# A hybrid decoder layer on one core: the three attention patterns are combined in another tile and a step later, and one sample row moves from the projection to the output stage

## The chip, the core and the metric

The kernel runs on one core of a Trainium2 chip. The core has five engines with a queue each: TensorE (PE in the profile, with its weight loads as PEld), VectorE (DVE), ScalarE (ACT), GpSimd (POOL), and SyncE (SP), which here issues nearly all DMAs. Each queue is worked off in order: an instruction, or a DMA issue, that waits holds up everything behind it on its engine. The metric is the device time of one execution in microseconds (us).

## What is computed

One layer over a prompt of 4096 positions (model width 1024) and 8 sample sequences of 4 new tokens each. Cut to what matters here:

```
q,k,v,g_att,x_lru,g_lru = split(x @ w_in)              # one input projection
for (window, dilation) in (128,1), (512,4), (2048,16): # 8 heads of 64, 129 keys each
    o_i, m_i, den_i = windowed attention, keys gathered by stride
w_i   = den_i * exp(m_i - max m);  y_att = sum(w_i * o_i) / sum(w_i)
h     = RG-LRU scan over a width-4 convolution of x_lru
y     = LayerNorm(alpha * x + [y_att*silu(g_att) ; h*silu(g_lru)] @ w_out)
sample tokens: the same, with 2048 cached K and V rows per sequence
```

## The kernel before

The program is written out in order by hand, with four stages. Matrix products of full accuracy are made of three matmuls on a high and a low part.

**Projection** (`phase1`, to about 580 us). For each of 8 pieces of 512 positions, q and k are made in four groups each (`qk_group`, 24 matmuls into one PSUM bank, emptied by ACT at L204 and DVE at L205), then v. After each group `decode_step` adds a piece of work for the sample tokens: the cached keys of one sequence and one pattern are loaded (`dec_load`, 1 MB, or 256 KB for the stride-1 pattern p = 2), multiplied by q on DVE (L375), summed (L380) and saved. `early` = 5 of the 8 sequences are done here, 15 pieces, one every 1.6 groups. `early` also says how many are left for the output stage.

**Attention** (`phase2`, to about 1475 us). 384 steps; a unit of 48 steps does one pair of heads over half the prompt. A unit has four stretches of 512 positions, nb = 0 to 3. A step issues scores (L562, L563), transposes (L582) of the step two before, and products with v (L598), with about four matmuls of another projection (`filler`) between. For the strides 4 and 16, q is gathered by POOL three steps ahead (`gather_q`, L512, tile `qg`, four buffers). When a stretch is complete, a chain of work follows for it, each piece at a lag in steps (`k.lag`): the softmax statistics go out to DRAM (`stats_out`, tiles s4d, s1d) and come back in another layout (`stats_in`, tile ac), DVE makes the weights (`weights`, `weights_b`), they go out (`weights_c`, wd), come back spread over all partitions (`spread`, tile gb, L657, one buffer), and POOL combines (`combine`): five operations of 128x512 spread over four steps, the first at L670, the others run from the step loop at L855. Then `store` (L674) writes the result to DRAM (ad), from gb, by a DMA that POOL issues. `spread` waits on SP until gb is free. The o of the stride-16 pattern lies in u16 (two buffers), that of the strides 4 and 1 in the tiles u1 and u2.

**Recurrence** (`phase3`, to about 1950 us) is not touched.

**Output** (`phase4`). 32 blocks of 48 matmuls (L1341), 8 ticks apart; `at(tick, ...)` sets the order of all else between them. Here the remaining sequences' keys are multiplied (L1494) and summed (L1498), from tick `k_start` on, `k_step` ticks each, and for each of two groups of four sequences a softmax `soft1` to `soft6` runs from `soft_at`: `soft2` transposes the scores on PE into the tile ds (L1507), `soft3` and `soft4` work on DVE and ACT (L1515 to L1526), `soft5` transposes back on PE (L1531). `tail_mm` puts the last recurrent state into PSUM under the same tag ds, and `tail_out` copies it out on ACT.

Of the kernel before, what the change touches and what calls it, by code (L numbers as in the profile page):

```python
# [23 lines left out]
SPAN = 512  # L24
# [6 lines left out]
class Kern:  # L31
# [125 lines left out]
    def phase1(self, xs_ctx):  # L157
# [227 lines left out]
        for n, (b, p) in enumerate([(b, p) for b in range(self.early) for p in (2, 0, 1)]):  # L385
            g = 1.6 * n
            for d, f in ((0, dec_load), (1.6, dec_mul), (2.4, dec_sum), (3.4, dec_save)):
                decode.setdefault(int(g + d), []).append((f, b, p))
            if p == 2:
                decode.setdefault(int(g + (0.2 if b else 0)), []).append((row_q, b))  # L390
        order = dec_mul, row_q, dec_sum, dec_save, dec_load
# [60 lines left out]
    def phase2(self):  # L452
# [137 lines left out]
        def back(x):  # L590
# [10 lines left out]
            if x.b == 3:  # L601
                if x.pat == 0:
                    nc.scalar.copy(x.unit.u16.rearrange("p (i r) -> p r i", r=16)[:, 4 * x.a:4 * x.a + 4],
                                   o.rearrange("p (r i) -> p r i", r=4))
                else:
                    t = up.tile([128, SPAN], F32, tag=f"u{x.pat}", name="u", bufs=1 + x.pat)
                    if x.pat == 1:
                        nc.scalar.copy(t.rearrange("p (m r) -> p r m", r=4), o.rearrange("p (r m) -> p r m", r=4))
                    else:
                        nc.scalar.copy(t, o)  # L610
                    x.unit.u[x.pat, x.a] = t
# [14 lines left out]
        def weights(un, nb):  # L626
            r = slice(nb * 32, nb * 32 + 32)
            ac = un.ac[r].rearrange("p k a h s -> p s k (a h)")
            w = sp.tile([128, 3, 32], F32, tag="w", name="w")
            m = sp.tile([128, 32], F32, tag="wm", name="wm")  # L630
            un.w[nb] = w, m
# [4 lines left out]
        def weights_b(un, nb):  # L636
            r = slice(nb * 32, nb * 32 + 32)
            ac = un.ac[r].rearrange("p k a h s -> p s k (a h)")
            w, m = un.w.pop(nb)
            g = sp.tile([128, 3, 2, 16], F32, tag="wg", name="wg")  # L640
            nc.vector.tensor_mul(ac[:, 1], w[r], ac[:, 1])
# [19 lines left out]
        def combine(un, nb):  # L661
            s, gb = slice(nb * SPAN, (nb + 1) * SPAN), un.gb[nb]
            e = nc.gpsimd
            for k, (f, o, y) in enumerate(((e.tensor_mul, 1, un.u[1, nb]), (e.tensor_mul, 0, un.u16[:, s]),
                                           (e.tensor_mul, 2, un.u[2, nb]), (e.tensor_add, 0, gb[:, 1]),
                                           (e.tensor_add, 0, gb[:, 2]))):
                if k:
                    defer(min(k, 3), f, gb[:, o], gb[:, o], y)
                else:
                    f(gb[:, o], gb[:, o], y)  # L670
            defer(3, store, un, nb)

        def store(un, nb):
            nc.gpsimd.dma_start(out=dap(self.ad, un.c * 128 * SEQ + un.st0 * ST + nb * SPAN, [[SEQ, 128], [1, SPAN]]),  # L674
                                in_=un.gb.pop(nb)[:, 0])

# [8 lines left out]
        def gate_mul(th, p, t, j):  # L685
            nc.vector.scalar_tensor_tensor(th, th, 1.0, p, op0=ALU.add, op1=ALU.mult)
            freed[0] += 1
            defer(1, gate_store, th, t, j)

# [655 lines left out]
    def phase4(self):  # L1345
# [258 lines left out]
        at(10.4, tables2)  # L1604
        at(12, tail_mm)
        at(13, tail_out)
        start = {b: 8 * b for b in range(n_b)}
# [70 lines left out]
def tile_hymba_dilated_attn_rglru(ctx, tc, ins, outs):  # L1678
    k = Kern(ctx, tc, ins, outs)
    k.pr = 0.2, 5.5, 7.0  # L1680
    k.p2 = 6, 9, 5, 1, 1, 3, 4, 3, 6, 11, 12, 15, 19, 24, 24, 24, 24, 17, 381, 387, 3.95
    k.kl, k.lag, k.f0, k.wl, k.fill_rate = k.p2[:7], k.p2[7:13], k.p2[13:18], k.p2[18:20] + (2,), (k.p2[20],) * 8
# [11 lines left out]
    k.e0, k.e1, k.e2, k.smp = 4, (2,), (9,), (5, 14)  # L1694
    k.early, k.k_start, k.k_step, k.soft_at, k.v_step = 5, 16.0, 24.0, (12.0, 112.0), (24.0, 22.0)
    xs = k.xs_ctx = ExitStack()
# [34 lines left out]
```

## Time and profile before

| | us |
|---|---|
| median of 3 runs (lowest, highest) | 2373.68 (2371.04, 2378.28) |
| the profiled execution | 2381.04 |
| its span, first to last instruction | 2379.3 |
| PE busy in it | 2202.8 (93%) |
| DVE busy | 1417.2 (60%) |
| ACT busy | 1091.8 (46%) |
| POOL busy | 528.7 (22%) |

The mean granted TensorE clock was 0.963 of 2.4 GHz; it stands either at 2.4 or at 1.2 GHz, so a mean below 1 says in which share of a stretch it was down. The profiled execution is 7.4 us above the median of the three runs. The span is a chain of four stages, so what is won in one shifts all that follow; a share over the whole span says little about a stage.

### The profile page before, as it was taken

To read this page: it belongs to the slowest core of one execution; us is meant where nothing else is said; L and a number is where in the kernel's file an instruction comes from. 1 tells how busy PE (TensorE), PEld (TensorE's weight loads), DVE (VectorE), ACT (ScalarE), POOL (GpSimd) and SP (SyncE) were. 2 spreads that over 40 slices of the span, in tenths; PEclk is the share of its full clock that TensorE was granted. 3 is DMA by queue.
4 is the path that set the end of the run, shared out by engine and by line. 5 is a ranking of instruction groups with operands and counts; after the bars stand their busy time and mean duration, and the time that the engine had idled before them with its cause. 6 is when DMAs were issued, how large, how long until landed. Compare 5 with 4: busy or idle time off the path is not lost.

```text
span 2379.3 us, 42567 instructions
## 1 busy us (share of the span) xinstructions
PE 2202.8 (93%) x15274; PEld 1903.2 (80%) x15274; DVE 1417.2 (60%) x3544; ACT 1091.8 (46%) x2819; POOL 528.7 (22%) x499
## 2 busy tenths in 40 slices
PE   6999999999799889989998988699999989999998
PEld 5887778888688779878887977699999976777776
DVE  4355553322366767656665745477878878855555
ACT  3211212222466557656665765376777752122221
POOL 1000000000337375564746475200000000000000
PEclk9999999999899999989999988899999999999999
DMA  6867776647957877777687855445555557655531
GB/s 175 255 231 222 253 231 221 203 169 222 237 130 182 182 194 176 197 186 183 176 195 194 177 160 141 142 153 151 168 164 187 164 177 282 219 198 185 203 131 58
DMA packets 325491, 444.68 MB, mean 187 GB/s; under 512 B 60836, under 2 KB 196004, under 8 KB 320160
## 3 DMA queue, kind: packets, MB, share of 16 engines
q1 hardware_dynamic: 322560, 433.04, 62.8%
q0 software_dynamic: 2720, 8.92, 1.1%
q8 instruction: 122, 2.00, 0.4%
q14 instruction: 89, 0.73, 0.1%
HBM read 306.04 MB, written 135.85 MB: 186 GB/s over the span
## 4 chain that ended last, share of the span: by engine, by line
PE 60%; DMA 14%; POOL 6%; DVE 5%; issue 3%; ACT 3%; SPq 2%; ACTq 0%; POOLq 0%; DVEq 0%
PE po L1341 15%; PE o L598 4%; PE pt L582 4%; DMA gb<-wd 4%; PE pp L190 4%; POOL gb L855 3%; POOL qg L512 3%; PE s L562 2%; PE pg L1019 2%; PE pg L1021 2%; PE pg L1020 2%; PE xl L140 2%; PE xl L144 2%; PE xl L142 2%; PE pp L317 2%
## 5 line engine op out<-in xcount | busy, mean ns | idle before, releaser
L512 POOL CAST qg<-S 128x512 fp32r<-128x512 f32 x256 | 277.0, 1102 | 639.8 <-DMA S<-qd 501.3
L1341 PE MATMUL po<-S,mx 128*128 128x512 f32 x1536 | 370.9, 401 | 4.0 <-DVE S L129 3.5
L1341 PEld LDWEIGHTS po<-S,mx 128*128 128x128 f32 x1536 | 290.1, 190 | 88.9 <-issue 11.2
L569 DVE CUSTOM_DVE_ANT_0 sm<-s,mask 128x256 f32<-128x256 f32 (+1 forms) x768 | 269.7, 389 | 101.7 <-PE s L563 86.5
L573 ACT ACTIVATE sm<-sm,st 128x256 f32<-128x256 f32 (+1 forms) x512 | 251.6, 493 | 166.0 <-DVE st L569 131.8
L586 DVE COPY pts<-pt 128x512 f32<-128x512 f32 x228 | 156.9, 688 | 158.6 <-PE pt L582 156.6
L582 PE MATMUL pt<-ident,sm 128*128 128x128 f32 x1368 | 230.9, 288 | 0.3 <-ACT sm L573 0.2
L598 PE MATMUL o<-pts,v 128*64 128x128 f32 x2736 | 202.3, 289 | 23.5 <-DMA v<-vd 22.4
L562 PE MATMUL s<-S,qg 128*128 128x256 f32 x512 | 164.1, 340 | 48.4 <-POOL qg L512 39.6
L598 PEld LDWEIGHTS o<-pts,v 128*64 128x64 f32 x2736 | 152.3, 142 | 52.9 <-DMA v<-vd 25.2
L190 PE MATMUL pp<-S,xh 128*128 128x512 f32 x768 | 179.4, 394 | 12.8 <-DVE stg L205 6.3
L582 PEld LDWEIGHTS pt<-ident,sm 128*128 128x128 f32 x1368 | 155.6, 144 | 36.0 <-issue 17.7
L190 PEld LDWEIGHTS pp<-S,xh 128*128 128x128 f32 x768 | 145.3, 190 | 45.4 <-DVE stg L205 7.2
L316 PE MATMUL pp<-xh,S 128*128 128x512 f32 x448 | 177.2, 396 | 3.6 <-ACT xh L114 3.6
L317 PE MATMUL pp<-xh,S 128*128 128x512 f32 x448 | 176.2, 393 | 1.6 <-DVE xh L115 1.6
L318 PE MATMUL pp<-xh,S 128*128 128x512 f32 x448 | 175.3, 391 | 0.0
L573 ACT ACTIVATE sm<-sm,ac 128x128 f32<-128x128 f32 (+1 forms) x256 | 114.3, 448 | 104.1 <-DVE ac L569 103.1
L707 PE MATMUL f<-xh,S 128*128 128x256 f32 x512 | 149.3, 292 | 5.2 <-DMA xh<-xtd 5.2
L140 PE MATMUL xl<-xh,S 128*128 128x256 f32 x512 | 147.6, 288 | 6.1 <-DMA xh<-xtd 4.1
L562 PEld LDWEIGHTS s<-S,qg 128*128 128x128 f32 x512 | 102.6, 200 | 59.3 <-POOL qg L512 52.6
L144 PE MATMUL xl<-xh,S 128*128 128x256 f32 x512 | 147.3, 288 | 2.6 <-DVE S L129 2.1
L712 PE MATMUL f<-xh,S 128*128 128x256 f32 x512 | 148.7, 290 | 0.0
(289 smaller groups left out, 5106.7 us busy)
## 6 DMA issues: line engine op xcount, KB each, us to landing
xh<-xtd SPq DMA_DIRECT2D x256, 256.0 KB
S<-qd SPq DMA_DIRECT2D x128, 256.0 KB
xtd<-xh SPq DMA_DIRECT2D x56, 512.0 KB
gb<-wd SPq DMA_DIRECT2D x64, 384.0 KB
v<-vd SPq DMA_DIRECT2D x264, 64.0 KB
S<-kd SPq DMA_DIRECT2D x64, 256.0 KB
xr<-in_x_prompt_dram SPq DMA_DIRECT2D x32, 512.0 KB
arena<-in_cache_v_dram SPq DMA_DIRECT2D x16, 1024.0 KB
```

Of the source, the lines that this page charges most:

```text
L140: nc.tensor.matmul(out, wh, xh, start=(c == 0), stop=False)
L144: nc.tensor.matmul(out, wl, xh, start=False, stop=(c == k - 1))
L190: nc.tensor.matmul(p, l, m, start=(c == 0 and a + b == 0), stop=(c == 7 and (a, b) == ((1, 0) if j < 2 else (0, 1))))
L316: nc.tensor.matmul(ps, wh, xh, start=(c == 0), stop=False)
L317: nc.tensor.matmul(ps, wh, xl, start=False, stop=False)
L512: nc.gpsimd.tensor_copy(o, q.bitcast(F32))
L562: nc.tensor.matmul(s[:, h], q_ap(x, h, 0), k, start=True, stop=False)
L569: nc.vector.tensor_tensor_reduce(x.sm[:, h, o], s[:, h, i], self.mask[:, x.pat, o], -0.125, 3e38, ALU.add, ALU.min, x.stat[:, h, 0:1])
L573: nc.scalar.activation(x.sm[:, h, o], x.sm[:, h, o], AF.Exp, bias=x.stat[:, h, 0:1], scale=-1.0, accum_out=x.stat[:, h, 1:2])
L582: nc.tensor.transpose(p[:, h, kb], x.sm[:, h, kb * 128:(kb + 1) * 128], self.ident)
L598: nc.tensor.matmul(o[h * 64:(h + 1) * 64, x.b * 128:(x.b + 1) * 128], v[:, h * 64:(h + 1) * 64], x.pt[:, h, kb], start=(kb == kbs[0]), sto ...
L1341: self.nc.tensor.matmul(ps[j], l, self.Wo[j][c][:, s], start=(c == 0 and s == 0 and l is mh), stop=(c == 7 and l is ml))
```

## The change

In the attention stage the combination is formed in u16 (its slice of 512 positions) instead of gb, and the store reads u16; gb is last read by the second addition. Three lags are one step longer: `stats_in` 7 (6), `spread` 16 (15), `combine` 20 (19). The tile u1 has three buffers instead of two, and three small tiles of the weights one instead of two. `gate_store` comes two steps after `gate_mul` instead of one. In the projection, four sequences (12 pieces) are decoded instead of five, one piece every two groups, the multiplication one group after the load. In the output stage four sequences' keys remain instead of three, from tick 10, every 22 ticks (16, every 24); the two softmaxes begin at 14 and 114 (12 and 112); `tail_mm` and `tail_out` go from 12 and 13 to 60 and 61.

```diff
@@ phase1
-            g = 1.6 * n
-            for d, f in ((0, dec_load), (1.6, dec_mul), (2.4, dec_sum), (3.4, dec_save)):
+            g = 2 * n
+            for d, f in ((0, dec_load), (1, dec_mul), (2, dec_sum), (3, dec_save)):
...
@@ phase2, back
-                    t = up.tile([128, SPAN], F32, tag=f"u{x.pat}", name="u", bufs=1 + x.pat)
+                    t = up.tile([128, SPAN], F32, tag=f"u{x.pat}", name="u", bufs=3)
@@ weights (wm and, in weights_b, wg in the same way)
-            w = sp.tile([128, 3, 32], F32, tag="w", name="w")
+            w = sp.tile([128, 3, 32], F32, tag="w", name="w", bufs=1)
...
@@ combine, store
-            s, gb = slice(nb * SPAN, (nb + 1) * SPAN), un.gb[nb]
-            e = nc.gpsimd
-            for k, (f, o, y) in enumerate(((e.tensor_mul, 1, un.u[1, nb]), (e.tensor_mul, 0, un.u16[:, s]),
-                                           (e.tensor_mul, 2, un.u[2, nb]), (e.tensor_add, 0, gb[:, 1]),
-                                           (e.tensor_add, 0, gb[:, 2]))):
+            gb, e = un.gb.pop(nb), nc.gpsimd
+            o = un.u16[:, nb * SPAN:(nb + 1) * SPAN]
+            for k, (f, *a) in enumerate(((e.tensor_mul, gb[:, 1], gb[:, 1], un.u[1, nb]), (e.tensor_mul, o, o, gb[:, 0]),
+                                         (e.tensor_mul, gb[:, 2], gb[:, 2], un.u[2, nb]),
+                                         (e.tensor_add, o, o, gb[:, 1]), (e.tensor_add, o, o, gb[:, 2]))):
...
             nc.gpsimd.dma_start(out=dap(self.ad, ...),
-                                in_=un.gb.pop(nb)[:, 0])
+                                in_=un.u16[:, nb * SPAN:(nb + 1) * SPAN])
@@ gate_mul
-            defer(1, gate_store, th, t, j)
+            defer(2, gate_store, th, t, j)
@@ phase4
-        at(12, tail_mm)
-        at(13, tail_out)
+        at(60, tail_mm)
+        at(61, tail_out)
@@ numbers (k.lag is the 8th to the 13th of k.p2)
-    k.p2 = 6, 9, 5, 1, 1, 3, 4, 3, 6, 11, 12, 15, 19, 24, 24, 24, 24, 17, 381, 387, 3.95
+    k.p2 = 6, 9, 5, 1, 1, 3, 4, 3, 7, 11, 12, 16, 20, 24, 24, 24, 24, 17, 381, 387, 3.95
-    k.early, k.k_start, k.k_step, k.soft_at, k.v_step = 5, 16.0, 24.0, (12.0, 112.0), (24.0, 22.0)
+    k.early, k.k_start, k.k_step, k.soft_at, k.v_step = 4, 10.0, 22.0, (14.0, 114.0), (24.0, 22.0)
```

What this moves on SP, around the first combination of a unit (wd: weights out, ac: statistics of the next stretch in, gb: the spread, L484 the v of stride 4, L446 the next q). Before:

```order
L649 DMA wd<-wg 32x6x16
L75 DMA xh<-xtd 128x512
L623 DMA ac<-s4d 32x64
L623 DMA ac<-s1d 32x64
L657 DMA gb<-wd 64x3x512 x2
L484 DMA v_8429<-vd 32x4x128 x4
L446 DMA S_77<-qd 64x2x512 x4
```

And in the changed kernel:

```order
L649 DMA wd<-wg 32x6x16
L75 DMA xh<-xtd 128x512
L623 DMA ac<-s4d 32x64
L623 DMA ac<-s1d 32x64
L484 DMA v_8405<-vd 32x4x128 x4
L657 DMA gb<-wd 64x3x512 x2
L446 DMA S_77<-qd 64x2x512 x4
```

The four loads of v have passed in front of the spread; for nb = 2 and 3 two loads at L477 do so in the same way.

On POOL, at the same place in the first unit (qg: gathers for PE, gb, u: the combination), before:

```order
L512 CAST qg<-S_77 128x512 x10
L670 TENSOR_TENSOR gb<-gb,u 128x512
L512 CAST qg<-S_77 128x512
L855 TENSOR_TENSOR gb<-gb,u_4250 128x512
L512 CAST qg<-S_77 128x512
L855 TENSOR_TENSOR gb<-gb,u 128x512
L855 TENSOR_TENSOR gb<-gb 128x512 x2
L674 DMA ad<-gb 128x512
```

And in the changed kernel:

```order
L512 CAST qg<-S_77 128x512 x11
L670 TENSOR_TENSOR gb<-gb,u 128x512
L512 CAST qg<-S_77 128x512
L855 TENSOR_TENSOR u_4229<-u_4229,gb 128x512
L855 TENSOR_TENSOR gb<-gb,u 128x512
L855 TENSOR_TENSOR u_4229<-u_4229,gb 128x512 x2
L674 DMA ad<-u_4229 128x512
```

One gather more stands ahead of the first multiplication, one fewer behind it, and the store reads u16 (u_4229).

On PE, at the beginning of the output stage (pf: tail_mm, ds: soft2, dt: soft5, po: the blocks). Before, between the second and the third block:

```order
L1341 MATMUL po<-S_79,mx 128x512
L1571 MATMUL pf<-ident,fin 12x128 x4
L1507 MATMUL ds<-ident,SC_22102 128x128
L1507 MATMUL ds<-ident,SC_22103 128x128
L1507 MATMUL ds<-ident,SC_22104 128x128
L1509 MATMUL ds<-ks,qe 128x32 x4
L1341 MATMUL po<-S_77,mx 128x512
```

(the rows at L1531 and L1532 follow after that third block), and in the changed kernel, between the third and the fourth:

```order
L1341 MATMUL po<-S_79,mx 128x512
L1507 MATMUL ds<-ident,SC_22081 128x128
L1507 MATMUL ds<-ident,SC_22082 128x128
L1507 MATMUL ds<-ident,SC_22083 128x128
L1509 MATMUL ds<-ks,qe 128x32 x4
L1531 MATMUL dt<-ident,dP 128x128 x3
L1532 MATMUL dt<-ident,dP 32x128
L1341 MATMUL po<-S_77,mx 128x512
```

The third block, which stood between ds and dt, has passed in front of both.

## Rows read from the trace of the kernel before

**Rows 1.** Busy us by stretch (matmuls behind x), granted clock, DMA share, GB/s:
```profile
150.00:360.00 210.00, 198.49 (x850) 159.68 (x849) 112.79 (x105) 37.71 (x55) 0.00 (x0) 0.99 0.72 233
700.00:1460.00 760.00, 688.90 (x6425) 620.02 (x6425) 496.28 (x1866) 482.83 (x1608) 445.70 (x406) 0.95 0.74 180
980.00:1020.00 40.00, 39.88 (x403) 36.60 (x402) 28.89 (x106) 27.81 (x93) 10.50 (x10) 1.00 0.86 206
1980.00:2100.00 120.00, 118.38 (x553) 86.29 (x551) 98.86 (x136) 25.38 (x55) 0.00 (x0) 1.00 0.68 240
```

**Rows 2.** Waits of PE, 700 to 1460: us in total, times, longest:
```profile
PE s L562 <- POOL qg L512: 39.6, 24, 4.7
PE o L598 <- DMA v<-vd: 22.4, 12, 6.6
```

**Rows 3.** Waits of POOL, same stretch:
```profile
POOL gb L670 <- DMA gb<-wd: 169.9, 21, 19.6
```

**Rows 4.** Waits of the DMA queue SP, same stretch:
```profile
SPq L657 <- DMA ad<-gb: 81.6, 19, 9.2
SPq L657 <- DMA wd<-wg: 32.5, 13, 5.8
```

**Rows 5.** Timeline 1066 to 1085, POOL, SP (start, us, instruction, idle before):
```profile
1066.18 2.62 POOL L855 TENSOR_TENSOR gb<-gb 128x512 f32<-128x512 f32 x2
...
1069.10 0.58 POOL L674 DMA_DIRECT2D ad<-gb  x1 [0.30 <-POOL gb L855]
...
1075.77 1.24 SPq L657 DMA_DIRECT2D gb<-wd  x2
...
1082.94 1.26 POOL L670 TENSOR_TENSOR gb<-gb,u 128x512 f32<-128x512 f32 x1 [8.14 <-DMA gb<-wd]
...
1084.15 1.04 POOL L512 CAST qg<-S 128x512 fp32r<-128x512 f32 x1
```

**Rows 6.** Timeline 1015 to 1023, a unit's first combination:
```profile
1015.08 1.23 SPq L657 DMA_DIRECT2D gb<-wd  x2
1016.41 1.97 SPq L484 DMA_DIRECT2D v<-vd  x4
...
1022.21 1.26 POOL L670 TENSOR_TENSOR gb<-gb,u 128x512 f32<-128x512 f32 x1 [16.54 <-DMA gb<-wd]
```

**Rows 7.** Timeline of PE, first and last of four waits there:
```profile
810.30 0.38 PE L562 MATMUL s<-S,qg 128*128 128x256 f32 x1 [4.69 <-POOL qg L512]
...
1451.50 0.39 PE L562 MATMUL s<-S,qg 128*128 128x256 f32 x1 [2.75 <-POOL qg L512]
```

**Rows 8.** Waits of PE and of DVE, 150 to 360:
```profile
PE pp L190 <- DVE stg L205: 6.3, 2, 3.2
...
DVE dk L375 <- DMA dk<-in_cache_k_dram: 20.7, 8, 5.7
```

**Rows 9.** Timeline 1960 to 2000, PE and DVE:
```profile
1964.42 0.69 PE L1507 MATMUL ds<-ident,SC 128*128 128x128 f32 x2 [9.65 <-ACT fo L1575]
...
1969.74 13.66 PE L1341 MATMUL po<-S,mx 128*128 128x512 f32 x48
...
1974.80 0.18 DVE L1516 TENSOR_TENSOR dP<-ds,mn 128x32 f32<-128x32 f32 x1
...
1978.89 0.43 DVE L1526 TENSOR_SCALAR dP<-dP,dr 128x416 f32<-128x416 f32 x1
...
1983.60 11.49 PE L1341 MATMUL po<-S,mx 128*128 128x512 f32 x48
```

**Rows 10.** Groups of DVE, 1960 to 2100: count, busy us, mean ns:
```profile
L1498 DVE TENSOR_REDUCE SC<-arena 128x32 f32<-128x2048 f32 x9 | 20.2, 2249 | 0.0
...
L1494 DVE TENSOR_TENSOR arena<-arena,qb 128x2048 f32<-128x2048 f32 x6 | 13.7, 2279 | 0.0
...
L1330 DVE SCALAR_TENSOR_TENSOR mx<-A,mx 128x256 fp32r<-128x256 f32 x20 | 7.1, 417 | 0.0
```

More of the change, by code (lines that the diff above doesn't have):

```diff
@@ L385, in phase1 @@
         for n, (b, p) in enumerate([(b, p) for b in range(self.early) for p in (2, 0, 1)]):
-            g = 1.6 * n
-            for d, f in ((0, dec_load), (1.6, dec_mul), (2.4, dec_sum), (3.4, dec_save)):
+            g = 2 * n
+            for d, f in ((0, dec_load), (1, dec_mul), (2, dec_sum), (3, dec_save)):
                 decode.setdefault(int(g + d), []).append((f, b, p))
             if p == 2:
-                decode.setdefault(int(g + (0.2 if b else 0)), []).append((row_q, b))
+                decode.setdefault(g, []).append((row_q, b))
         order = dec_mul, row_q, dec_sum, dec_save, dec_load
@@ L628, in weights @@
             ac = un.ac[r].rearrange("p k a h s -> p s k (a h)")
-            w = sp.tile([128, 3, 32], F32, tag="w", name="w")
-            m = sp.tile([128, 32], F32, tag="wm", name="wm")
+            w = sp.tile([128, 3, 32], F32, tag="w", name="w", bufs=1)
+            m = sp.tile([128, 32], F32, tag="wm", name="wm", bufs=1)
             un.w[nb] = w, m
@@ L639, in weights_b @@
             w, m = un.w.pop(nb)
-            g = sp.tile([128, 3, 2, 16], F32, tag="wg", name="wg")
+            g = sp.tile([128, 3, 2, 16], F32, tag="wg", name="wg", bufs=1)
             nc.vector.tensor_mul(ac[:, 1], w[r], ac[:, 1])
@@ L661, in combine @@
         def combine(un, nb):
-            s, gb = slice(nb * SPAN, (nb + 1) * SPAN), un.gb[nb]
-            e = nc.gpsimd
-            for k, (f, o, y) in enumerate(((e.tensor_mul, 1, un.u[1, nb]), (e.tensor_mul, 0, un.u16[:, s]),
-                                           (e.tensor_mul, 2, un.u[2, nb]), (e.tensor_add, 0, gb[:, 1]),
-                                           (e.tensor_add, 0, gb[:, 2]))):
+            gb, e = un.gb.pop(nb), nc.gpsimd
[3 more added lines that the diff above has]
+                                         (e.tensor_add, o, o, gb[:, 1]), (e.tensor_add, o, o, gb[:, 2]))):
                 if k:
-                    defer(min(k, 3), f, gb[:, o], gb[:, o], y)
+                    defer(min(k, 3), f, *a)
                 else:
-                    f(gb[:, o], gb[:, o], y)
+                    f(*a)
             defer(3, store, un, nb)
```

## Prediction

> **What bounds the kernel now.** I read the busy times by stretch first, because the stages have different limits. The reader should look at three numbers of each row of [rows 1]: how long PE is busy, at which granted clock, and how many matmuls it got through. In a quiet piece of the attention stage PE does 403 matmuls in 40 us at clock 1.00, 10.1 per us. Over most of the stage, 700 to 1460, it does 6425 in 760 us, 8.5 per us. PE is idle there for 760 - 688.9 = 71 us, and the clock of 0.95 costs about 0.05 x 760 = 38 us more: after an idle time TensorE goes on at 1.2 GHz for a while. So some 109 us of this stretch are not needed for matmuls, and this is the largest reserve that the change touches.
>
> Who holds PE up is in its waits [rows 2]: 39.6 us for q gathered by POOL and 22.4 us for v from DRAM, together 62 of the 71. POOL gathers late because the first multiplication of a combination, which stands ahead of the next gathers in its queue, waits for gb: 169.9 us in 21 cases [rows 3]. Why gb comes late is in the waits of SP [rows 4]: the spread is held up there for 81.6 us, 19 times, until the store of the combination before has landed, since that store reads gb, and for 32.5 us until the weights have landed. What SP has behind the spread, the loads of v first, is late with it.
>
> [Rows 5] show one turn of this. The two additions end at 1068.80, the store is issued at 1069.10, the spread only at 1075.77, and POOL takes up the next combination at 1082.94 after 8.14 us of idle.
>
> **The change part by part.** All terms are against the profiled execution, 2381.04 us.
>
> *Combination in u16.* gb is free when the second addition ends, not when the store has landed. In [rows 5] that is 1068.80 instead of 1075.77, 7.0 us; over the 19 cases 81.6 / 19 = 4.3 us. The spread does not get all of it, since four loads of v now stand in front of it on SP, 1.97 us of issue [rows 6]. It lands about 2.3 us sooner, and the combination starts one step later with one gather more already done. A step is some 19 matmuls (four for scores, up to four transposes, up to eight for o, four of the filler), 19 / 10.1 = 1.9 us. So POOL, which waits 169.9 / 21 = 8.1 us on average, should wait about 4. PE has up to four gathered q in hand, some four steps, and a wait of 4 us should seldom reach it.
>
> The first combination of each unit is different. There gb has long been free, and the spread waits for the weights [rows 6]; POOL's 16.54 us of idle stand there. PE is held up at four of these eight places, 4.69 us at the first and 2.75 us at the last [rows 7]; four times their mean is about 15 us. The extra gather gives PE one step more; v's loads are issued while SP would wait for the weights anyway. I leave 10 of these 15 us. Of the other 39.6 - 15 = 25 us of PE's waits for POOL I leave 8. Together 22 us are saved.
>
> *Loads of v ahead of the spread.* They no longer wait for it. Of 22.4 us I leave 7, so 15 us are saved.
>
> *Clock.* If 22 + 15 = 37 of 71 us of idle go, I take the same share of the 38 us: 20 us.
>
> *Given back.* POOL itself becomes tight. In the part of a unit where it gathers for every step it has three combinations of 5 x 1.3 us and a store issue of 0.6 us, and twenty gathers of 1.04 us [rows 5]: 21 + 21 = 42 us. PE needs 22 steps x 1.9 = 42 us for the same steps. With no reserve left there, part of the wait stays: I take 1.5 us in each of the eight units, 12 us.
>
> Attention: 22 + 15 + 20 - 12 = 45 us saved. Bounds: all of it, 109 us; and on the other side a loss of 5 us, if the spreads land later by the issue of the v loads and the later combination just makes up for it.
>
> Here a rule speaks against the change. SP's queue shows what the old order cost, but in [rows 5] the store had landed before the spread began; now both are under way at once. The Trainium skill, "DMA: Bandwidth & Descriptors", section "Issuing engines are not separate DMA queues", says that DMAs started by different engines end up on the same 16 DMA engines and interleave. By it the store's 256 KB (128 x 512 values), at the 180 GB/s of [rows 1] 1.5 us, would delay the spread, and the 2.3 us would shrink to 0.8. No row of this trace shows the two together. This is the first rival below.
>
> *The other edits of this stage* I cost at nothing: the third u1 buffer only takes a wait from ACT that none of PE's rows names; the weights' tiles with one buffer are used once in eight steps and read one step later; the statistics come in one step later, four steps before DVE reads them; `gate_store` is behind no one.
>
> *Projection.* Three pieces of 2.28 + 2.25 us on DVE (tiles of the same size as those of [rows 10]) and 2.25 MB of loads go, and the other twelve are spread evenly. PE is idle for 210 - 198.5 = 11.5 us there [rows 1], 6.3 us of it because DVE empties a bank late [rows 8]. I take half of the 11.5, 6 us. Bounds: 12 us gained, or 5 lost, since the multiplication now always comes one group after its load, and DVE already waits 20.7 us for such loads [rows 8].
>
> *Head of the output stage.* Two things happen. The 9.65 us in which ds waits for the copy of `tail_mm`'s result [rows 9] go. But `soft5` now follows `soft2` on PE with no block between, so PE waits through the softmax. In the trace the third block, 13.66 us long after the idle time, lies over that softmax (1974.80 to 1978.89 + 0.43 on DVE). Afterwards DVE has in front of the softmax, beside what it had, two multiplications (2.28 each), one sum (2.25) and four splits (4 x 0.42 = 1.7): 8.5 us. So the softmax begins at about 1974.8 + 8.5 = 1983.3, ends 4.5 us later at 1987.8, dt takes 0.6, and the fourth block starts at 1988.4 instead of 1983.60 [rows 9], 4.8 us later. PE has then idled for some ten us, and this block takes 13.66 rather than 11.49 us, 2.2 more. Together 7 us lost. Bounds: 10 us gained, if the idle before the third block goes and the softmax waits for nothing; 21 us lost, if besides these 7 all of the moved row's DVE work, 3 x (2.28 + 2.25) = 13.6 us, comes on top. I take 7: in 1980 to 2100 DVE is busy for 98.86 of 120 us [rows 1], so the row still fits beside PE. The few transposes of `tail_mm` only move.
>
> Sum: 2381.04 - 45 - 6 + 7 = 2337. The profiled execution is 7.4 us above the median, so **2330 us**; its own range is 2310 to 2350.
>
> **The rivals.**
> 1. *The wait turns into transfer time.* Spread, store and loads of v share the DMA engines, and gb lands hardly sooner; only the extra step and the v loads help, and the clock with them. Then attention saves about 15 of v, a fourth of the 39.6, 10, and 13 of clock, less the 12: 26, and the time is 2381 - 26 - 6 + 7 - 7 = 2349. For it: DMA share 0.74 over the stretch and 0.86 in the quiet piece [rows 1]. Against it: in that quiet piece PE runs at full rate.
> 2. *The idle pieces become short enough that TensorE keeps 2.4 GHz.* All 38 us of clock come back, and POOL's lead covers the 12: 22 + 15 + 38 = 75, so 2300. For it: the quiet piece, with 0.1 us of idle in 40, holds 1.00 [rows 1]. Against it: the first combinations stay late.
> 3. *The spread was not what set PE's waits*, the weights before it are (32.5 us in [rows 4], and the longest wait of POOL, 19.6). Then stalls only move, attention gains nothing, and the projection's 6 and the output's 7 cancel: 2375.
> 4. *Slower: DVE becomes the bound of the output stage.* Place: the four rows' keys from the softmax on. Price: 7 + 13.6 = 21 us. It decides the sign once the two stages before save less than 21; with 5 of attention and 6 of the projection the time is 2374 + 21 - 11 = 2384. For it: DVE's 82%. Against it: the saving in attention must be nearly absent too.
>
> **How the numbers follow.** Forecast 0.48, rival 1 0.25, rival 2 0.10, rival 3 0.08, rival 4 0.09. A measurement of this kernel tells 0.3%, about 7 us, from no change: faster is below 2366.6, slower above 2380.8. Forecast and rivals 1 and 2 give faster, 0.83; rival 3 the same, 0.08; rival 4 slower, 0.09. The range 2295 to 2375 takes in the first three cases and touches the fourth; beyond it lie rival 4 and the far end of rival 2.
>
> **What would show it.** Right: SP's waits of the spread for ad are gone, POOL's wait for gb falls from 169.9 to under 100 us, PE's waits for qg and v in the attention stage fall from 62 to about 25, the clock of that stretch rises from 0.95 to about 0.97, and the stage is about 45 us shorter. In the output stage a wait of PE at L1531 for the softmax, of about ten us, stands where the wait at L1507 was. Wrong: POOL's wait for gb stays above 140 us though SP no longer waits for the store (rival 1), or SP waits as long for wd instead (rival 3); or PE's waits for DVE after 1980 grow to more than 5 us (rival 4). If the first four blocks of the output stage end sooner than before, the term of 7 us is wrong.

## The result, and the profile after

The changed kernel takes 2336.43 us (median of 6 executions, 2331.30 to 2345.26), the kernel before 2373.43 us (6 executions, 2371.04 to 2378.28): a ratio of 0.9845, 95% interval 0.9824 to 0.9865. 37 us are gone, of the 43 forecast. The profiled execution took 2335.18 us, its span 2333.5.

First the same stretches as in [rows 1], the last two moved to where their work now stands: busy time with the number of matmuls, the granted clock, DMA share and GB/s.
```profile
150.00:360.00 210.00, 204.23 (x844) 160.46 (x843) 100.31 (x98) 37.76 (x55) 0.00 (x0) 0.96 0.68 217
700.00:1400.00 700.00, 660.84 (x6322) 597.78 (x6320) 488.19 (x1830) 472.16 (x1574) 434.41 (x395) 0.97 0.78 192
1929.00:2049.00 120.00, 111.44 (x516) 80.68 (x517) 106.59 (x144) 27.78 (x58) 0.00 (x0) 0.95 0.73 263
```
The attention stage gets through 6322 / 700 = 9.03 matmuls per us instead of 8.45. In the projection PE is *busier* and yet does fewer matmuls, 844 instead of 850. The clock is 0.96 instead of 0.99, but that is not all: e7 below shows that waiting lies inside PE's busy time. At the head of the output stage PE does 516 instead of 553.

PE's waits from 700 to 1417 answer [rows 2], POOL's and SP's from 621 to 1417 [rows 3, 4]:
```profile
PE s L562 <- POOL qg L512: 24.5, 19, 3.0
PE s L562 <- DVE st L569: 8.2, 8, 3.1
PE o L598 <- DMA v<-vd: 5.2, 1, 5.2
```
```profile
POOL gb L670 <- DMA gb<-wd: 103.4, 18, 15.0
```
```profile
SPq L657 <- POOL u L855: 26.8, 11, 4.8
...
SPq L657 <- DMA wd<-wg: 9.5, 5, 3.9
```
The spread's wait for the store is gone; what it waits for now is POOL's second addition. PE's waits for q and v together are 29.7 us instead of 62.0 (about 25 were forecast). A wait for DVE's statistics (L569), which no term of the forecast names, is at 8.2 us where it was 4.3 from 700 to 1460.

One turn, to be held against [rows 5] (SP and POOL in order of time: start, us, instruction, idle before):
```profile
1037.25 1.23 SPq L657 DMA_DIRECT2D gb<-wd  x2
1037.52 0.58 POOL L674 DMA_DIRECT2D ad<-u  x1 [0.30 <-POOL u L855]
...
1045.14 1.28 POOL L670 TENSOR_TENSOR gb<-gb,u 128x512 f32<-128x512 f32 x1 [1.98 <-PE pt L582]
```
The spread starts 0.27 us ahead of the store's issue, not 6.67 us behind it (1069.10 to 1075.77), and POOL's idle before the next combination is 1.98 us, for PE, not 8.14 us for gb.

The first combination of a unit is still late (compare [rows 7]): of PE's waits at these places the first and the last are
```profile
808.25 0.58 PE L562 MATMUL s<-S,qg 128*128 128x256 f32 x1 [3.02 <-POOL qg L512]
...
1410.92 0.39 PE L562 MATMUL s<-S,qg 128*128 128x256 f32 x1 [2.06 <-POOL qg L512]
```

The head of the output stage, PE alone, against [rows 9]:
```profile
1909.79 13.03 PE L1341 MATMUL po<-S,mx 128*128 128x512 f32 x48 [6.57 <-DVE xr L1395]
1922.66 0.74 PE L1507 MATMUL ds<-ident,SC 128*128 128x128 f32 x3
...
1935.93 0.87 PE L1531 MATMUL dt<-ident,dP 128*128 128x128 f32 x3 [11.71 <-DVE dP L1526]
...
1936.66 13.16 PE L1341 MATMUL po<-S,mx 128*128 128x512 f32 x48
```
`soft5` stands right behind `soft2` and PE waits 11.71 us through the softmax, as forecast. Not forecast was the 6.57 us that the third block waits for DVE to empty a bank.

The key row that moved is in DVE's groups from 1909 to 2049, against [rows 10] (count, busy us, mean ns):
```profile
L1498 DVE TENSOR_REDUCE SC<-arena 128x32 f32<-128x2048 f32 x11 | 24.8, 2256 | 0.0
L1494 DVE TENSOR_TENSOR arena<-arena,qb 128x2048 f32<-128x2048 f32 x8 | 18.2, 2278 | 0.0
```
Each instruction costs what it did; there are two more of each.

Stage lengths by PE's marks (projection: last L316; attention: from there to the last L582; recurrence: first to last L1019; output: first to last L1341), for both kernels and all experiments below:

| kernel | projection ends | attention | recurrence | output | median us |
|---|---|---|---|---|---|
| before | 589.5 | 871.8 | 461.6 | 443.4 | 2373.4 |
| before, profiled again (e12) | 587.8 | 865.0 | 461.9 | 443.7 | 2373.2 |
| changed | 590.8 | 825.8 | 455.3 | 449.5 | 2336.4 |
| e1 attention edits | 586.2 | 825.4 | 455.7 | 443.8 | 2324.5 |
| e2 u16 alone | 586.7 | 844.0 | 454.5 | 442.4 | 2342.2 |
| e3 steps alone | 584.9 | 849.9 | 458.3 | 444.4 | 2355.6 |
| e4 changed, soft5 later | 593.2 | 825.7 | 455.9 | 447.0 | 2339.4 |
| e5 e1, late tail | 589.5 | 829.7 | 455.9 | 443.9 | 2328.6 |
| e6 changed, early tail | 592.1 | 827.0 | 457.4 | 447.8 | 2338.2 |
| e7 changed, later multiplication | 572.8 | 829.8 | 456.1 | 449.4 | 2320.7 |
| e8 e1, later multiplication | 572.6 | 824.1 | 455.3 | 444.2 | 2311.7 |
| e9 e8, softmax two places later | 573.1 | 827.4 | 455.7 | 453.9 | 2315.7 |
| e11 e9, six rows | 575.4 | 825.3 | 455.8 | 440.9 | 2309.9 |
| e13 changed, softmax at 12 | 592.4 | 822.1 | 457.3 | 445.5 | 2331.8 |

Means over profiles, with their number: attention 868.4 (2) to 826.2 (10, all with the whole attention edits), recurrence 461.8 (2) to 456.0 (the same 10); by their own code in these stages projection 587.4 (6) to 592.1 (4), output 443.7 (7) to 448.9 (3; the place of the tail is left out of account). Profiles of the same code differ by up to 5 us in the projection and 2 us in the output stage. The changes are -42.2, -5.8, +4.7 and +5.2: -38, against -37 between the medians.

### The profile page after: what moved, and what is told of

It reads as the page before. It is cut to its first block, busy times and chain, and to the rows that moved or that the text cites. A ratio compares the mean times of both kernels' runs of the same rounds, so it can differ in the third digit from the quotient of the medians.

```text
span 2333.5 us, 42473 instructions
## 1 busy us (share of the span) xinstructions
PE 2193.2 (94%) x15274; PEld 1891.7 (81%) x15274; DVE 1424.5 (61%) x3544; ACT 1093.0 (47%) x2819; POOL 529.9 (23%) x499
## 4 chain that ended last, share of the span: by engine, by line
PE 69%; DMA 13%; DVE 5%; POOL 5%; SPq 4%; issue 3%; ACT 2%; ACTq 0%; POOLq 0%; DVEq 0%
PE po L1341 15%; PE o L598 6%; PE pp L190 6%; PE pt L582 6%; DMA dk<-in_cache_k_dram 3%; PE s L562 3%; PE s L563 3%; PE pg L1019 2%; PE pg L1021 2%; PE pg L1020 2%; PE pp L316 2%; PE pp L317 2%; PE pp L318 2%; PE xl L144 2%; PE xl L140 2%
## 5 line engine op out<-in xcount | busy, mean ns | idle before, releaser
L1341 PE MATMUL po<-S,mx 128*128 128x512 f32 x1536 | 371.9, 402 | 10.4 <-DVE xr L1395 7.1
L1341 PEld LDWEIGHTS po<-S,mx 128*128 128x128 f32 x1536 | 290.3, 191 | 95.8 <-issue 17.3
L569 DVE CUSTOM_DVE_ANT_0 sm<-s,mask 128x256 f32<-128x256 f32 (+1 forms) x768 | 269.5, 389 | 83.4 <-PE s L563 72.7
L582 PE MATMUL pt<-ident,sm 128*128 128x128 f32 x1368 | 227.6, 285 | 0.1
L598 PE MATMUL o<-pts,v 128*64 128x128 f32 x2736 | 197.5, 285 | 6.6 <-DMA v<-vd 5.2
L316 PE MATMUL pp<-xh,S 128*128 128x512 f32 x448 | 179.6, 401 | 4.0 <-ACT xh L114 3.5
L582 PEld LDWEIGHTS pt<-ident,sm 128*128 128x128 f32 x1368 | 153.9, 142 | 34.3 <-ACT sm L573 17.2
L317 PE MATMUL pp<-xh,S 128*128 128x512 f32 x448 | 178.7, 399 | 1.7 <-DVE xh L115 1.7
L318 PE MATMUL pp<-xh,S 128*128 128x512 f32 x448 | 177.0, 395 | 0.0
L205 DVE TENSOR_TENSOR stg<-pp,stg 128x512 fp32r<-128x512 f32 x56 | 50.9, 912 | 159.2 <-ACT stg L204 159.0
```

What stands on the lines that cost most here:

```text
L316: nc.tensor.matmul(ps, wh, xh, start=(c == 0), stop=False)
L317: nc.tensor.matmul(ps, wh, xl, start=False, stop=False)
L318: nc.tensor.matmul(ps, wl, xh, start=False, stop=(c == 7))
L569: nc.vector.tensor_tensor_reduce(x.sm[:, h, o], s[:, h, i], self.mask[:, x.pat, o], -0.125, 3e38, ALU.add, ALU.min, x.stat[:, h, 0:1])
L582: nc.tensor.transpose(p[:, h, kb], x.sm[:, h, kb * 128:(kb + 1) * 128], self.ident)
L598: nc.tensor.matmul(o[h * 64:(h + 1) * 64, x.b * 128:(x.b + 1) * 128], v[:, h * 64:(h + 1) * 64], x.pt[:, h, kb], start=(kb == kbs[0]), sto ...
```

## The experiments

**e1: the attention edits alone.** Before, with everything of the diff between L603 and L688 and the new `k.p2`; the sample rows, `soft_at` and the tail as before.

> The kernel before with the edits of the attention stage alone; projection and output stage as before. Theory (the stage gains by its own edits, and the rest follows from it): the attention stage ends some 45 us sooner, the recurrence is some 6 us shorter as in the changed kernel, the output stage is as before. Against the changed kernel the projection's +1.3 us and the output stage's +6.1 us are missing: about 2329 us, ratio to before 0.981. Rival (part of the gain of the attention stage comes from the state that the changed projection leaves to it): the stage gains less than 35 us, above 2340 us.

Measured: 2324.46 us (2322.43 to 2334.84), before beside it 2371.51; ratio 0.9811 (0.9787 to 0.9834). Attention 825.4 us: the whole gain of the stage comes from its own edits. It is 12 us below the changed kernel, more than the 7 expected: the rest of the change costs time. (The two intervals just overlap; that the projection and the output stage are the longer ones in the changed kernel shows in the stage lengths of all profiles.)

**e2: the combination in u16 alone**, steps and buffers as before.
```diff
-                f(gb[:, o], gb[:, o], y)
+                f(*a)          # operands as in the changed combine
-                            in_=un.gb.pop(nb)[:, 0])
+                            in_=un.u16[:, nb * SPAN:(nb + 1) * SPAN])
```


> The kernel before with the combination formed in u16 alone: no later step, no third buffer. Theory (the spread's wait for the store's landing, 81.6 us in 19 cases, is what made gb late): SP's wait for ad is gone, POOL's wait for gb falls from 169.9 us to about 110, PE's waits for POOL fall by half, and the attention stage gains 20 to 30 us: about 2350 us, ratio 0.99. Rival (the combination's later step and the v loads ahead of the spread do the work): under 8 us gained, above 2365 us.

**e3: the later steps and the third buffer alone**, the combination still in gb.
```diff
-    k.p2 = 6, 9, 5, 1, 1, 3, 4, 3, 6, 11, 12, 15, 19, 24, ...
+    k.p2 = 6, 9, 5, 1, 1, 3, 4, 3, 7, 11, 12, 16, 20, 24, ...
-tag=f"u{x.pat}", name="u", bufs=1 + x.pat)
+tag=f"u{x.pat}", name="u", bufs=3)
-            defer(1, gate_store, th, t, j)
+            defer(2, gate_store, th, t, j)
```


> The kernel before with the later combination, the later statistics and the third buffer, but the combination still formed in gb. Theory: the spread still waits for the store, about 80 us in all, POOL's wait for gb falls only by the one step, and v, which now stands ahead of the spread, no longer waits: PE's 22 us of waits for v go, and the stage gains 10 to 20 us, about 2358 us. Rival (the store's wait is hidden by one more step of lead): 35 us or more are gained, under 2338 us.

Measured: e2 2342.18 us, ratio 0.9877 (0.9863 to 0.9892); e3 2355.63 us, ratio 0.9935 (0.9918 to 0.9953). PE's waits in the attention stage of e2 and then of e3:
```profile
PE s L562 <- POOL qg L512: 24.7, 15, 4.4
PE o L598 <- DMA v<-vd: 20.3, 9, 7.5
```
```profile
PE s L562 <- POOL qg L512: 37.6, 30, 3.0
...
PE o L598 <- DMA v<-vd: 8.7, 2, 7.3
```
The two halves do separate work. Forming the result in u16 takes 15 us from PE's waits for POOL and leaves v; the later steps take 14 us from the waits for v and leave POOL. In e3 the spread still waits 90.9 us for the store:
```profile
SPq L657 <- DMA ad<-gb: 90.9, 18, 10.7
```
One expectation of e2 failed: POOL's wait for gb fell only to 161.4 us (23 cases), not to 110. The waits for gb go down with the steps (118.7 in e3, 103.4 with both), and are a poor measure of what PE gains. Against the mean of before, the stage gains 24 us in e2 and 19 in e3, and 43 in e1: the parts add up.

**e4: a block between soft2 and soft5 in the changed kernel.**
```diff
-    k.soft = 0.49, 2.0, 5.0, 5.5, 9.5, 11.0, 12.75, 4.77, 7.0
+    k.soft = 0.49, 2.0, 5.0, 5.5, 10.1, 11.0, 12.75, 4.77, 7.0
```


> The changed kernel with soft5 one block later, so that a block of the output projection stands between soft2 and soft5 again. Theory (the head of the output stage is late because PE waits 11.7 us through the softmax and runs its next block at half clock): that wait goes and the block after it is some 2 us shorter; a small wait for the softmax's sum may come. The output stage is some 9 us shorter, about 2327 us, ratio to the changed kernel 0.996. Rival (DVE, not PE, carries these 100 us, so that the wait only moves): no change, within 3 us of the changed kernel.

Measured: 2339.41 us (2335.61 to 2341.12), ratio to before 0.9867 (0.9851 to 0.9884); nothing gained. PE at that head:
```profile
1926.76 11.50 PE L1341 MATMUL po<-S,mx 128*128 128x512 f32 x48
1938.65 0.52 PE L1531 MATMUL dt<-ident,dP 128*128 128x128 f32 x3 [0.39 <-DVE dP L1526]
...
1947.00 1.89 PE L1551 MATMUL do<-vs,Z 32*8 32x512 f32 x8 [7.72 <-DVE Z L1537]
```
The block covers the softmax, and the next link is late instead: the copy of dt into Z, with DVE's block work ahead of it, makes PE wait 7.72 us. The wait moved; 2.5 us of the output stage are saved, no more than the profiles differ by. The rival is right.

**e5: the late tail alone**, on e1; **e6: the early tail** in the changed kernel.
```diff
-        at(12, tail_mm)
-        at(13, tail_out)
+        at(60, tail_mm)
+        at(61, tail_out)
```


> The kernel with the attention edits alone (2324 us), and tail_mm and tail_out at 60 and 61 as in the changed kernel; five sample rows in the projection as before. It splits the output stage's loss between the moved tail and the moved sample row. Theory (the row that moved costs, because DVE's work on its keys stands ahead of the softmax and of the copies; the moved tail frees PE of 9.8 us of waiting): the first four blocks of the output stage end earlier than with the tail at 12, by 2 to 9 us, and the time is 2316 to 2322 us. Rival (with the tail gone, soft5 comes with no block between and PE waits through the softmax; that alone makes the output stage 6 us longer): about 2330 us.

> The changed kernel with tail_mm and tail_out back at 12 and 13: attention edits and four sample rows, one piece per group, in the projection. Theory (the projection is 5 us longer because the multiplication one group after its load waits for the load and the groups at the start of a piece then fall to half clock; the output stage pays for the row that moved): projection ends at about 591 us, output stage 5 or more us longer than with five rows: 2334 to 2340 us. Rival (the tail, not the row, costs in the output stage): projection as late, output stage as with five rows, about 2330 us.

Measured: e5 2328.58 us, ratio 0.9815 (0.9795 to 0.9834), output 443.9 us; e6 2338.21 us, ratio 0.9856 (0.9834 to 0.9878), output 447.8 us. The tail neither costs nor gives. Both expectations of e5 were wrong: its time is near the rival's, but its output stage is not longer. By the intervals it can't be told from e1, and its profile is of an execution of 2333.22 us, 5 above the median, with a later end of the projection (589.5) and a longer attention stage (829.7). e6 came out as its theory had it (projection's end 592.1, time 2338), with 4.1 us of the 5 in the output stage. With the tail gone, ds waits as long as before, now told as a wait for another instruction of ACT:
```profile
1915.99 0.66 PE L1507 MATMUL ds<-ident,SC 128*128 128x128 f32 x2 [9.41 <-ACT mx L1329]
```
`ds` reads SC and not mx. A row of DVE in the same profile shows the scores landing just then, when ds starts:
```profile
1915.63 1.43 DVE L1330 SCALAR_TENSOR_TENSOR mx<-B,mx 128x256 fp32r<-128x256 f32 x4 [0.67 <-DMA SC<-scd]
```
So behind the copy of [rows 9] the scores' load was nearly as late: before, the same row of DVE starts at 1963.01, 1.4 us ahead of ds. That PE waits for this load is read from the two rows, not tried.

**e13: the softmax's place alone**, in the changed kernel; **e12: before, profiled again.**
```diff
-    k.early, k.k_start, k.k_step, k.soft_at, k.v_step = 4, 10.0, 22.0, (14.0, 114.0), (24.0, 22.0)
+    k.early, k.k_start, k.k_step, k.soft_at, k.v_step = 4, 10.0, 22.0, (12.0, 112.0), (24.0, 22.0)
```


> The changed kernel with the softmax of the sample rows at 12 and 112 again instead of 14 and 114 (four rows, one piece per group and the late tail stay). It splits the head of the output stage between the softmax's new place and the row that moved. Theory (the place of the softmax, which puts soft5 right behind soft2's block, makes the 11.7 us; the row costs little): the wait at dt goes, a wait of some 10 us for the scores comes back at ds, the output stage takes 443 to 446 us instead of 449.5. Rival (the row's multiplications on DVE, ahead of the softmax, cost the 6 us): 448 us or more.

> The kernel before, unchanged, profiled a second time. The first profiled execution took 2381 us against a median of 2373.5; its projection ended at 589.5 us and its recurrence took 461.6 us, where six kernels with the same code in these stages and the edits elsewhere showed 584.9 to 589.5 and 454.5 to 458.3. Theory (the 6 us by which the recurrence seems shorter after the change are a draw of that one execution): recurrence 454 to 459 us, projection's end 585 to 590, attention stage 868 to 874. Rival (the order that the old attention stage leaves behind makes the recurrence longer): 460 us or more again.

Measured: e13 2331.83 us (median of three executions, 2331.36 to 2341.21; a fourth took 7301.52 us, which nothing here explains), ratio 0.9845 (0.9814 to 0.9876). Its output stage takes 445.5 us, as the theory said, with waits at ds of 9.5 and 6.0 us:
```profile
PE ds L1507 <- ACT mx L1329: 9.5, 1, 9.5
PE ds L1507 <- DVE SC L1501: 6.0, 1, 6.0
```
So of the +5.2 us some 3.4 are the softmax's new place (448.9 - 445.5), and 1.8 the row that moved: its multiplications on DVE stand ahead of the mask at L1501 (6.0 instead of 2.8 us in e8). This rests on one profile of e13, where profiles of the same code differ by up to 2 us; in the medians these few us can't be told.

e12 took 2373.15 us. Its recurrence took 461.9 us again: the rival is right, the 6 us are no draw. Its attention stage, 865.0, was shorter than expected: some 7 us of the first profile's 871.8 were chance. Where the 6 us come from shows in DVE at the start of the recurrence, first before (e12), then changed:
```profile
1500.63 0.69 DVE L1153 TENSOR_TENSOR pa<-pa,pb 128x512 f32<-128x512 f32 x1 [6.44 <-DMA pb<-gd]
1501.24 0.69 DVE L967 TENSOR_TENSOR uh<-u,uh 128x512 fp32r<-128x512 f32 x1
```
```profile
1461.13 0.69 DVE L1153 TENSOR_TENSOR pa<-pa,pb 128x512 f32<-128x512 f32 x1 [4.54 <-DMA pb<-gd]
1461.74 0.68 DVE L967 TENSOR_TENSOR uh<-u,uh 128x512 fp32r<-128x512 f32 x1
```
PE waits for uh of L967 there. It stands in DVE's queue behind L1153, which waits for two loads (L1149) of results of the attention stage. What these loads wait for on SP, in e12 and then in the changed kernel:
```profile
SPq L1149 <- DMA ad<-gb: 9.7, 1, 9.7
```
```profile
SPq L1149 <- POOL u L855: 7.3, 1, 7.3
```
The pattern is that of the spread: in e12 the first load is issued 2.4 us behind the issue of the last store (1496.84, 1494.46), when that has landed, in the changed kernel 0.3 us ahead of it (1456.59, 1456.86), when POOL's second addition ends. e2, with u16, is like the changed kernel (454.5 us of recurrence), e3, without it, waits 9.5 us for the store (458.3). From the first L1019 (1454.5 and 1418.3) it is 46.7 us to L967 before and 43.4 after, 3.3 us; the rest of the 6 is not traced, and that the loads go into space that gb had is not shown.

**e7 and e8: the decode multiplication one group later**, in the changed kernel and on e1.
```diff
-            for d, f in ((0, dec_load), (1, dec_mul), (2, dec_sum), (3, dec_save)):
+            for d, f in ((0, dec_load), (2, dec_mul), (3, dec_sum), (4, dec_save)):
```
```diff
-            for d, f in ((0, dec_load), (1.6, dec_mul), (2.4, dec_sum), (3.4, dec_save)):
+            for d, f in ((0, dec_load), (2.4, dec_mul), (3.2, dec_sum), (4.2, dec_save)):
-                decode.setdefault(int(g + (0.2 if b else 0)), []).append((row_q, b))
+                decode.setdefault(int(g + (1.2 if b else 0)), []).append((row_q, b))
```


> The changed kernel with the decode multiplication two groups after its load instead of one (sum and save one later each). Theory (DVE's waits for the loaded piece, 50.9 us in 12 cases, make the x chunks late, and PE's many short waits for these put it at half clock at 245 to 260 and 320 to 330): the waits of DVE for dk fall under 15 us, these stretches hold 1.00, the projection ends 5 to 9 us sooner, the time is about 2329 us. Rival (DVE's busy time, not its waits, is what makes the chunks late): dk's waits go but the half clock stays and the projection ends within 2 us of 590.8; about 2336 us.

> The kernel with the attention edits alone (2324 us), with the decode multiplication, sum and save about one group later (2.4, 3.2 and 4.2 after the load instead of 1.6, 2.4 and 3.4; the row of q one later). Theory: DVE's waits for dk, 31.5 us in 9 cases, fall under 15 us, the two waits of PE for a bank of 3.7 us each shrink, and the projection ends 3 to 6 us sooner: about 2320 us. Rival (what delays the bank there is the 2.3 us each of DVE's work, wherever it stands): within 2 us of 2324 us.

Measured: e7 2320.66 us (2317.41 to 2324.36), ratio to before 0.9779 (0.9760 to 0.9799); e8 2311.74 us (2307.20 to 2315.02), ratio 0.9740 (0.9720 to 0.9760). Both theories named DVE's waits, rightly, and gave a third to a half of the size. DVE's waits for dk over the stage fell from 50.9 to 16.6 us in e7 (under 15 expected) and from 31.5 to 12.4 in e8. PE in the changed kernel, where a piece of 512 positions begins; L316 to L318 are the three matmuls on one x chunk:
```profile
242.23 0.39 PE L316 MATMUL pp<-xh,S 128*128 128x512 f32 x1
...
245.02 0.51 PE L316 MATMUL pp<-xh,S 128*128 128x512 f32 x1 [0.60 <-ACT xh L114]
...
247.06 0.54 PE L316 MATMUL pp<-xh,S 128*128 128x512 f32 x1 [0.58 <-ACT xh L114]
...
249.12 0.80 PE L316 MATMUL pp<-xh,S 128*128 128x512 f32 x1
249.84 0.80 PE L317 MATMUL pp<-xh,S 128*128 128x512 f32 x1
...
254.96 0.63 PE L316 MATMUL pp<-xh,S 128*128 128x512 f32 x1
...
256.24 0.63 PE L316 MATMUL pp<-xh,S 128*128 128x512 f32 x1
...
257.80 0.39 PE L317 MATMUL pp<-xh,S 128*128 128x512 f32 x1
```
DVE makes the chunks together with ACT, one after the other (transpose L111, ACT's rounding L114, difference L115), behind a multiplication that waited for its load:
```profile
235.19 2.29 DVE L375 TENSOR_TENSOR dk<-dk,qb 128x2048 f32<-128x2048 f32 x1 [3.41 <-DMA dk<-in_cache_k_dram]
237.40 0.71 DVE L111 STREAM_TRANSPOSE raw<-X 128x512 f32<-128x512 f32 x1
...
249.10 0.69 DVE L115 TENSOR_TENSOR xh<-raw,xh 128x512 fp32r<-128x512 f32 x1 [0.74 <-ACT xh L114]
...
251.14 0.69 DVE L115 TENSOR_TENSOR xh<-raw,xh 128x512 fp32r<-128x512 f32 x1 [0.73 <-ACT xh L114]
```
A chunk comes every 2.05 us, and from 243 to 255 us PE goes at just this pace: its L317 at 249.84 starts 0.05 us after DVE's L115 ends. The idle times told are at most 0.6 us and stop at 248; after that the waiting lies inside the longer records. The granted clock falls in the same stretch:
```profile
240.00:250.00 10.00, 8.08 (x25) 4.31 (x23) 6.32 (x11) 3.09 (x5) 0.00 (x0) 0.87 0.64 262
250.00:260.00 10.00, 9.80 (x25) 6.30 (x26) 3.62 (x6) 1.72 (x3) 0.00 (x0) 0.62 0.69 226
```
Where PE is full, such ten us hold 46 matmuls. But half clock is the smaller loss: three matmuls take 1.28 us by it (254.96 to 256.24), less than a chunk takes to come. The six chunks from 242.97 to 254.96 cost 12.0 us instead of 6 x 0.68 = 4.1, so 7.9 are lost to the pace of the chunks; the two that follow at half clock lose 1.2. In e7 the chunks come as slowly, but begin 17 us ahead of PE's first use (239.87) and are done by then:
```profile
222.71 0.69 DVE L111 STREAM_TRANSPOSE raw<-X 128x512 f32<-128x512 f32 x1
...
238.77 0.69 DVE L115 TENSOR_TENSOR xh<-raw,xh 128x512 fp32r<-128x512 f32 x1 [0.73 <-ACT xh L114]
```
The stretch 150 to 360 and DVE's waits in it, in e7:
```profile
150.00:360.00 210.00, 210.00 (x928) 173.87 (x927) 107.34 (x108) 44.11 (x63) 0.00 (x0) 1.00 0.70 227
```
```profile
DVE dk L375 <- DMA dk<-in_cache_k_dram: 9.6, 5, 3.2
```
In the changed kernel the same wait of DVE is
```profile
DVE dk L375 <- DMA dk<-in_cache_k_dram: 39.3, 10, 5.7
```
928 instead of 844 matmuls, at 928 / 210 = 4.42 per us, are 19 us; the projection ends 18 us sooner. DVE's time in that stretch is no smaller (107.34 against 100.31), so it is its waits, with the x chunks queued behind them, that starve PE. The clock of 0.96 can account for at most 0.04 x 210 = 8.4 of the 19 us, and in most of that time the chunks set the pace anyway.

**e9 and e11: a block for each link of the sample softmax**, on e8 with five and with six rows.
```diff
-    k.soft = 0.49, 2.0, 5.0, 5.5, 9.5, 11.0, 12.75, 4.77, 7.0
+    k.soft = 0.49, 2.0, 5.0, 5.5, 10.1, 11.0, 18.5, 4.77, 7.0
-    k.early, k.k_start, k.k_step, k.soft_at, ... = 5, 16.0, 24.0, (12.0, 112.0), ...
+    k.early, k.k_start, k.k_step, k.soft_at, ... = 5, 16.0, 24.0, (14.0, 114.0), ...   # e11: 6, 30.0
```


> The kernel with the attention edits and the later decode multiplication (2312 us, five sample rows, tail at 12), with the softmax of the first four rows two places later (soft_at 14 and 114, so that soft2 comes after the third block, as in the changed kernel), soft5 one block after it and the first products with v one block after that. Theory (PE's 9.4 + 2.8 us at the first transposes are the landing of the scores and DVE's mask, which a block can cover, and each later link of the chain gets a block of its own): these waits, and the ones of 11.7 and 7.7 us that took their place in the other orders, are all gone, a wait of some 6 us for DVE to empty the bank of the third block stays: the output stage is 5 to 9 us shorter, about 2305 us. Rival (DVE's work at this head is the bound, as in the try with soft5 alone): under 2 us gained, about 2311 us.

> The same with six sample rows in the projection instead of five, the next row of keys in the output stage at 30 instead of 16. Theory (a row of keys is 13.6 us of DVE work, which the projection can hide since PE is busy for all of it there, while at the head of the output stage DVE is late): the projection still ends within 2 us of 573 us, and the wait for the bank at the third block shrinks: 2 to 5 us less than with five rows. Rival (in the projection 18 pieces at 1.6 groups make the x chunks late again, with half clock): projection ends 4 us or more later, and the time is no less than with five rows.

Measured: e9 2315.73 us, ratio 0.9768 (0.9746 to 0.9789); e11 2309.91 us (2307.49 to 2311.93), ratio 0.9730 (0.9711 to 0.9748). e9 gained nothing on e8. The waits at ds, dt and Z of that head are gone, and its first 60 us hold 211 matmuls instead of 174. But new waits of 2.5 us (DVE's clearing of do) and 2.3 us (a load of v) stand later, and the blocks behind them take 13.4 and 14.1 us instead of 11.5, at a lower granted clock. The next 60 us, in e9 and then in e8:
```profile
1919.70:1979.70 60.00, 54.18 (x217) 38.14 (x216) 51.56 (x68) 12.23 (x29) 0.00 (x0) 0.86 0.68 250
```
```profile
1915.50:1975.50 60.00, 59.19 (x278) 42.76 (x277) 50.69 (x69) 11.58 (x28) 0.00 (x0) 1.00 0.68 243
```
Here 61 matmuls are lost, some 13 us, where the head gained 8; a further wait of 2.2 us at the second softmax costs some 4. That is most of the 10 us by which the output stage is longer than in e8, in a profile of an execution of 2324.78 us, 9 above e9's median. With six rows (e11) that stage is 440.9 us, the shortest of all, and the projection loses 2 to 3 us; the time is 6 us below e9, where 2 to 5 were expected. e11 and e8 can't be told apart by their intervals; both beat the changed kernel and e1.

## Why the prediction was right, and where not

**Attention: -45 forecast, -46.0 between the two profiles, -42.2 over all.** The mechanism is the one forecast: SP's waits of the spread for ad are gone. PE's waits for POOL fell by 15 us (22 less 12 forecast), those for v by 17 (15 forecast). The clock went from 0.95 to 0.97: 38 us of loss become 0.03 x 700 = 21, 17 saved where 20 were forecast. POOL's wait for gb ended at 103.4, a little over the bound of 100. e2 and e3 show that both edits were needed, as the two terms had it.

**Rival 1 (transfers) is there, and too small to decide.** From the end of the spread's issue to POOL's start on gb, where POOL waits for it, it took 5.47 us before (mean of 24) and 6.01 after (20). The mean hides two kinds: in the 9 of the 20 in which the store is issued within 1 us of the spread it is 6.69 us, in the other 11 it is 5.45 (medians 6.19 and 5.19). So where the two run at once the spread is 1.2 us late, most of the 1.5 that would have left 0.8, but over all only 0.5. The store pays as well: it lands 5.2 us after its issue (median) where it took 2.6, and the spread no longer waits for that. The Trainium skill, "DMA: Bandwidth & Descriptors", section "Issuing engines are not separate DMA queues", has it that such transfers interleave. The traces agree, by the 6.69 against 5.45 us.

**The other rivals.** Rival 2: the clock rose to 0.97, not to 1.00. Rival 3: SP's wait for the weights did not stay, it fell from 32.5 to 9.5 us. Rival 4: the only waits of PE for DVE in the output stage that grew are the two at its head told below.

**Projection: -6 forecast, +4.7 measured.** The failed step is "I take half of the 11.5". It takes PE's idle time for what can be won. That idle time did fall by half (11.5 to 5.8 us; the two waits for the bank of [rows 8] are gone), but the time did not follow: DVE's waits for the loaded keys grew from 20.7 to 39.3 us, the x chunks behind them came late, and PE waited for them inside its busy records, at half clock in part. The bound "5 lost", for a multiplication one group after its load, named the right wait. Counting matmuls in the stretch would have shown more: the kernel before does 850 where e7 does 928.

**Head of the output stage: +7 forecast, +5.2 measured.** The terms of the sum held: counted from the stage's first matmul the softmax begins 7.5 us later (8.5 forecast) and the fourth block 4.1 (4.8), and that block takes 1.7 us more (2.2). The wait at dt is as forecast (11.71, "some ten us"). Wrong was what the prediction says goes: the 9.65 us did not hang on `tail_mm`'s copy, since without it ds waits 9.41 (e5). They went because the third block came first, and that block came to a bank that DVE had not emptied (6.57 us). Neither enters the sum: in both traces DVE comes to the softmax straight from the work queued ahead of it, without idle time.

**Recurrence: nothing forecast, -5.8 measured.** It comes with the attention edits (e1, e2), and 3.3 us of it are the earlier loads told at e12; the rest is open. **The 7.4 us** taken off for the profiled execution were right: e12 found 6.8 of them in the attention stage.

The forecast of 2330 is 6 us low: 11 from the projection, 3 from attention, less 2 from the output stage and 6 from the recurrence. That it is so near is in part luck: the recurrence, which is in no term, makes up for half of the projection's miss.

## What to carry to other kernels

A buffer that is both a transfer's source and the next transfer's target ties the two together; writing the result into another tile unties them. Count matmuls per us in a stretch, not idle time alone: PE's busy records can hold waiting, as here, where 19 us were lost and 5.8 told as idle. An engine that reaches an instruction before its load has landed holds up all that is queued behind it, so look at what that is. A wait that goes uncovers the next link: list the whole chain, with what is queued ahead of each link on its engine, before counting the first as gained.

## What was not expected of the hardware

TensorE fell to half clock without any long idle time: between 243 and 248 us it did three matmuls every 2.05 us and waited in pieces of at most 0.6 us, and the granted clock was 0.87 and then 0.62 in the two stretches shown at e7. With the chunks there in time (e7) the stretch 150 to 360 holds 1.00. And a load that DVE reaches too early (39.3 us of waits) cost PE some 18 us, though PE never waited for that load itself.
